# First feed-forward output as seven half-size products, with its input sums made as the input is produced and the modulation sums spread anew

## The chip, the cores and the metric

The kernel runs on one core of one Trainium2 chip. Times are device microseconds (us) of that core, from one launch; lower is better. Clocks inside one profiled execution are counted from the start of its span. Engines are named as in the profile: PE (matrix), PEld (its weight loads), DVE (vector), ACT (scalar), POOL and SP (which here mostly issue DMAs).

## The reference

A two-layer trunk for 256 latent tokens and 256 context tokens of width 1024. Layer 0 mixes tokens with a bidirectional mLSTM, layer 1 with latent attention; each mixer is followed by a gated convolutional feed-forward. In layer 0 both streams are computed, in layer 1 only the latent one is read at the end.

```python
def _conv_ffn(h, w_in, conv_w, conv_b, w_out):
    gate, up = jnp.split(h @ w_in, 2, axis=-1)          # 1024 -> 2 x 2816
    return (jax.nn.silu(_dwconv(gate, conv_w, conv_b)) * up) @ w_out   # 2816 -> 1024
...
for i in range(DEPTH):                                   # DEPTH = 2
    ml = _modulation(c, ada_w[i], ada_b[i])              # six vectors of 1024 per condition
    mc = _modulation(c_ctx[None, :], ada_w[i], ada_b[i])
...
    x = _layer_norm(ALPHA * x + ml[2] * yl, ln_g[i, 0], ln_b[i, 0])
    f = _conv_ffn(_modulate(x, ml[3], ml[4]), ffn_w_in[i], ...)
    x = _layer_norm(ALPHA * x + ml[5] * f, ln_g[i, 1], ln_b[i, 1])
```

The change concerns the last product of layer 0's feed-forward, `(512 tokens x 2816) @ w_out (2816 x 1024)`, for both streams.

## The kernel before

Everything is float32, and each product is made of three matmuls on split operands. `split` turns a tile into a rounded high part (a cast on ACT, `L380`, or `L315` for weights) and a low part (a subtraction on DVE, `L381` or `L318`). `mm3` (`L375` to `L377`) then issues high x high, high x low and low x high into one PSUM tile. The pool of PSUM tiles has eight tiles of 128 x 512, all of one tag.

Weights come through the class `Stream`. `_plan` writes the fixed order of weight tiles (128 x 1024 at most, 512 KB), `_load` issues the DMA of the next one on SP into a ring of raw tiles, `_split` casts and subtracts it into one of three split tiles (`NB = 3`, tag `w`), and `use` hands it to the matmuls. So the split of tile number k waits until the matmuls of tile k-3 have ended. Tiles marked wide are split into tiles of the tag `u` instead, and do not wait for one of the three. From `bufs` on, later stages add further tags to the ring of raw tiles.

The stages, in the order PE runs them: `up` and `og` (projections), `v` (`w_v`, which already is made of seven half-size products in place of eight, with sums of the weights by `_sum` and sums of the input in `x_sums`), `qk` with the heads, `mout` (mixer output), `fin0` (first feed-forward product), `fout0` (its output), then `dkv`, `ukn`, `uv` and the rest of the attention, `aout`, `fin1`, `fout1`.

In `fin0`, `ffn_in` makes 22 pairs of PSUM tiles (gate and up), runs the convolution (`conv`: two ACT steps and two DVE steps), multiplies, and splits the result into the 22 tiles `act`, kept in SBUF. In `fout0`, `outmm` runs over these 22 tiles twice: first for the 256 context tokens (four PSUM tiles: two token blocks by two halves of the width), then for the 256 latent tokens. Each weight tile is thus loaded and split twice and serves 12 matmuls each time. While the latent half runs, the context half goes through residual, LayerNorm and transposes (`after0`, `ln_rows`, `ln_T`) one step per weight tile (`tick`). The last six weight tiles are wide; before them stands `mla_ctx`, which computes the context's `dkv` product from the normalized context (`hc`). After them the latent half goes through the same LayerNorm (`z` tiles, `zT` transposes) while PE runs `ukn` and `uv` of the context; then comes `dkv` of the latent half (`hl`).

The modulation vectors that are not needed at the start are computed on DVE in the background: `ada_all` yields one step at a time, each a multiply with a running sum over a 128 x 1024 tile (`junk<-ar,bc`, `L504`). 128 of these are spread over the stages by the rates `ADA_U` (`up`), `ADA_T` (`og`), `ADA_Q` (`qk`), `ADA_M` (`mout`), `ADA_F` (`fin0`), steps per weight tile.

A scheduler orders the instructions of each engine when the program is built, from the order of issue and its own estimates; at run time each engine works its queue in that order.

Of the kernel before, what the change touches and what calls it, by code (L numbers as in the profile page):

```python
# [7 lines left out]
F32 = mybir.dt.float32  # L8
# [6 lines left out]
D = 1024  # L15
# [23 lines left out]

VE = {1: (3, 0), 2: (3, 0), 3: (3, 0)}  # L40

ADA_U, ADA_T, ADA_Q, ADA_M, ADA_F = 1, 0.8, 1.6, 0.6, 1.3

# [10 lines left out]
TAIL = {"mout": 4, "fout0": 6, "aout": 7, "fout1": 6}  # L54
WIDE = {"mout": 5, "fout0": 6, "aout": 7, "fout1": 10}


def _stat(w, m, kt0, nkt):
# [10 lines left out]
def _plan():  # L69
    ids, order = {}, []  # L70

    def add(key, cols, wide=False):
        if key not in ids:
            ids[key] = (len(ids), cols)
        order.append((key, wide))

    for m in range(16):
        add(("up", m, 0), 1024)
    for s in range(4):
        for c in range(4):  # L80
# [36 lines left out]
    for k in range(8):  # L117
        add(("aout", 0, k), 1024, k >= 8 - WIDE["aout"])
    for p in range(NF):
        add(("fin1", p, 0), 1024, p < 2)  # L120
        add(("fin1", p, 1), 1024, p < 2)
    for k in range(NF):
        add(("fout1", 0, k), 1024, k >= NF - WIDE["fout1"])
    return ids, order


def _pack(i):
# [12 lines left out]
    for key, (n, cols) in ids.items():  # L140
# [4 lines left out]
            b = _mov(i["m_w_og"][0][:, a * 512:(a + 1) * 512], 2 * c, 2)  # L145
        elif kind == "gates":
            b = gz.reshape(16, 128, 16).transpose(1, 0, 2).reshape(128, 256)
        elif kind[0] == "v":

            x, y = {"v11": (0, 0), "vt1": (0, 1), "v21": (1, 0), "vt4": (1, 0)}.get(kind, (1, 1))  # L150
            q = i["m_w_v"][0][:, (2 * a + y) * 512:(2 * a + y + 1) * 512]
            b = np.concatenate([q[k * 128:(k + 1) * 128] for k in (4 * c + x, 4 * c + 2 + x)], axis=1)
        elif kind == "qk":
            b = _stat(i["m_w_qk"][0], a, 8 * c, 8)
        elif kind == "mout":
# [73 lines left out]
class Stream:  # L229


    def __init__(self, k, ids, order, ws):
        self.k, self.ids, self.order, self.ws = k, ids, order, ws
        self.n = len(order)
        self.nl = self.ns = self.nu = 0
        self.live, self.kept = [], []
        self.limit = self.n
        self.raw, self.hl, self.tags = {}, {}, {}
        self.nsum = 0

# [4 lines left out]
        self.bufs.append((keys.index(("fout0", 0, 8)), self.bufs[-1][1] + [("acc", 2)] * 2 + [("ar1", 1), ("junk", 1)]))  # L245
        self.bufs.append((keys.index(("aout", 0, 0)), self.bufs[-1][1] + [("ar", 2)] * 2))

    def ring(self, j):
# [13 lines left out]
    def _load(self):  # L262
        k, j = self.k, self.nl
        key = self.order[j][0]
        n, cols = self.ids[key]
        j0, ring = self.ring(j)
        tag, bufs = ring[(j - j0) % len(ring)]
        t = k.pool.tile([128, CW], F32, tag=tag, name="raw", bufs=bufs)
        if key[0] == "vt4":
            k.nc.sync.dma_start(t, k.t2d[key[1]][key[2]])  # L270
            k.nc.gpsimd.dma_start(t, self.ws[n], accum_op=ALU.add)
        elif key[0] != "vt2":
            k.nc.sync.dma_start(t[:, :cols], self.ws[n, :, :cols])
        self.raw[j] = t
        self.tags[j] = tag
        self.nl += 1

    def _sum(self, j):

        key = self.order[j][0]  # L280
        if key[0] == "vt1":
            nc, pin = self.k.nc, self.k.tc.keep_in_program_order
            t2, b11, b22, b12 = [self.raw[i] for i in range(j - 3, j + 1)]
# [4 lines left out]
    def _split(self):  # L288
# [24 lines left out]
            k.nc.vector.tensor_sub(v[:, :, 1], src, v[:, :, 0])  # L313
        else:
            k.nc.scalar.copy(h[:, :cols], src)  # L315
            if key[0] == "vt2":
                k.nc.scalar.dma_start(k.t2d[key[1]][key[2]], src)
            k.nc.vector.tensor_sub(l[:, :cols], src, h[:, :cols])  # L318
        self.hl[j] = (h, l)
        self.ns += 1  # L320
# [26 lines left out]
class K:  # L347
# [141 lines left out]
    def ada_bg(self, l, c, nconds):  # L489


        nc = self.nc
# [5 lines left out]
        for k in range(8):  # L498
            w = self.art.pop(0)
            self.ar_load()  # L500
            for j in range(nconds):
# [2 lines left out]
                nc.vector.scalar_tensor_tensor(o, w, 1.0, self.bc[j], op0=ALU.mult, op1=ALU.mult,  # L504
                                               accum_out=col[:, k, j:j + 1])
                yield
        b = self.smc("ada_c")[:, 48 * l + 8 * c:48 * l + 8 * c + 8].unsqueeze(2).to_broadcast([128, 8, nconds])
# [21 lines left out]
    def ada_all(self, items):  # L529
# [3 lines left out]
        for j in range(2):  # L533
# [4 lines left out]
        self.arq = [(l, c, k) for l, c in items for k in range(8)]  # L538
        self.art, self.nar = [], 0
        for _ in range(2):  # L540
            self.ar_load()
# [2 lines left out]
        for r in self.bc:  # L544
            nc.scalar.activation(r, r, AF.Silu)  # L545
        yield
        for l, c in items:
            yield from self.ada_bg(l, c, 2 if l == 0 or c < 2 else 1)
        self.bc = None


# [23 lines left out]
    def start_up(self):  # L575
# [5 lines left out]
        self.t2d = [[self.dr.tile([128, 1024], F32, name="t2d%d%d" % (p, j)) for j in range(4)] for p in range(2)]  # L581
# [700 lines left out]
    def ffn_in(self, l, hT, n, nt, pre=()):  # L1282
# [5 lines left out]
        for p in range(NF):  # L1288
# [16 lines left out]
            tmp = self.s2("fg")  # L1305
            self.conv(pss[0], [cw[:, j * NF + p:j * NF + p + 1] for j in range(3)], cb[:, p:p + 1], tmp, n)
            nc.vector.tensor_tensor(tmp[:, :n], tmp[:, :n], pss[1][:, :n], op=ALU.mult)
            a = self.u("act")
# [3 lines left out]
        return acts  # L1312


    def rms(self, ps, n, dst):
# [280 lines left out]
def build(tc, off, a, out):  # L1596
    es = ExitStack()
    with es:
# [4 lines left out]
        k.setup()  # L1603
        st.skip(NUP)
        k.start_up()
        k.bg2.append(k.ada_all(((0, 2),)))
        k.w_up()
        k.bg = [k.x_sums()]
        k.w_og()
# [1 line left out]
            k.step(k.bg2)  # L1611
        k.w_v()
        k.drain()
        k.bg2.append(k.ada_all(((0, 3), (0, 4), (0, 5), (1, 0), (1, 1), (1, 2), (1, 3), (1, 4), (1, 5))))
        gp = k.gates()
        S = None
        tt = None
# [64 lines left out]
        while k.bg2:  # L1682
            k.step(k.bg2)
        h0 = None
        act = lambda i: (acts[i][:, 0], acts[i][:, 1])
        pc = k.acc4()
        xr = k.res_load(x1d, 0)
        gate = k.bcast(k.gd[0, 5][1:2, :], "gate")
        k.outmm("fout0", range(NF), act, pc, 0, NF, 1)
        hcu = [k.u("hc") for _ in range(4)]  # L1690
        hc = lambda i: tuple(hcu[i // 2][:, n, (i % 2) * 256:(i % 2 + 1) * 256] for n in range(2))
        k.bg = [after0(pc, xr, gate, 0, 1, 1, 0, hc, None)]
        pl = k.acc4()
        xr = k.res_load(x1d, 2)
        gate = k.bcast(k.gd[0, 5][0:1, :], "gate")
        k.outmm("fout0", range(NF - TAIL["fout0"]), act, pl, 256, NF, 1)
        k.drain()
        kv0 = [x[0] for x in order].index(("ukn", 0, 0))
        st.limit = kv0 + PA
        k.rope_load()  # L1700
        k.mla_ctx(hc)
        hc = hcu = None
        k.outmm("fout0", range(NF - TAIL["fout0"], NF), act, pl, 256, NF, 1, True)
        acts = None
        hlu = [k.u("hl") for _ in range(4)]
        hl = lambda i: tuple(hlu[i // 2][:, n, (i % 2) * 256:(i % 2 + 1) * 256] for n in range(2))
        x2d = k.dr.tile([2, 128, D], F32, name="x2d")
        k.bg = [after0(pl, xr, gate, 1, 1, 1, 0, hl,
                       [x2d[0], x2d[1]])]
        k.tick(1)  # L1710
        st.pump(kv0 + PB)
        k.tick(1)
# [64 lines left out]
```

## Time and profile before

| | |
|---|---|
| median of 3 runs | 1394.01 us (1393.62 to 1394.03) |
| the profiled execution's own time | 1394.95 us |
| its span | 1393.2 us |
| PE busy | 1368.5 us, 98% |
| DVE busy | 1030.5 us, 74% |
| ACT busy | 694.2 us, 50% |
| mean granted PE clock | 0.997 |

The profiled execution took 0.94 us more than the median, and 1.75 us of it lie outside its span. The ends of matmuls are modelled, so the distance between two starts says more than a duration. In the views by stretch, each engine's busy time in a stretch is followed by its count of instructions, then come the PE clock, the share of the DMA engines and GB/s.

### The profile page before, as it was taken

Reading aid. Unit: us, or ns where it says so; the run is one execution under the profiler, and the core shown is the slowest. Engines: PE = TensorE matmul, PEld = TensorE weight load, DVE = VectorE, ACT = ScalarE, POOL = GpSimd, SP = SyncE. Lnnn points to the kernel's source line nnn. Section 1 sums busy time; section 2 is a strip of 40 time slices with the busy share of each in tenths; the row PEclk is TensorE's granted clock in tenths of the full one; section 3 lists DMA queues with packets and bytes.
Section 4 is the critical chain, followed back from the end, with each engine's and each line's share of the span. In section 5 each row is a group of like instructions: output and inputs, shape, how many; then the busy total and the mean of one; then the engine's idle time right before and its main releaser. Section 6 shows DMA issues by size and latency. Waiting matters only on the chain.

```text
span 1393.2 us, 19087 instructions
## 1 busy us (share of the span) xinstructions
PE 1368.5 (98%) x6969; PEld 1152.3 (83%) x6969; DVE 1030.5 (74%) x1627; ACT 694.2 (50%) x1161; POOL 107.6 (8%) x193
## 2 busy tenths in 40 slices
PE   7999999999999999999999999999999999999997
PEld 3788888888788888878798888888888998999986
DVE  6598657687688697789799777754567889777773
ACT  6585434445544545375654343333464667455560
POOL 0033000011011011110000000000000001000000
PEclk9999999999999999999999999999999999999999
DMA  9688748789655364656737677755565326357650
GB/s 337 225 276 298 263 158 242 243 289 289 228 196 209 110 230 153 222 195 212 252 138 238 225 243 241 251 183 181 187 209 179 137 99 213 108 189 226 210 182 31
DMA packets 91262, 288.97 MB, mean 207 GB/s; under 512 B 11288, under 2 KB 19736, under 8 KB 91168
## 3 DMA queue, kind: packets, MB, share of 16 engines
q1 hardware_dynamic: 69824, 224.29, 48.4%
q0 software_dynamic: 15296, 50.36, 11.5%
q10 hardware_dynamic: 6048, 13.11, 2.5%
q8 instruction: 54, 0.88, 0.3%
q14 instruction: 40, 0.33, 0.1%
HBM read 261.46 MB, written 26.26 MB: 207 GB/s over the span
## 4 chain that ended last, share of the span: by engine, by line
PE 91%; DVE 3%; ACT 2%; DMA 2%; issue 1%; SPq 0%; DVEq 0%; ACTq 0%
PE fin L375 9%; PE fin L376 9%; PE fin L377 9%; PE tok L375 6%; PE tok L377 6%; PE tok L376 6%; PE y L376 5%; PE y L377 5%; PE y L375 5%; PE qk L375 4%; PE qk L377 4%; PE qk L376 4%; PE up L375 2%; PE up L377 2%; PE up L376 2%; DMA raw<-in_ws 2%
## 5 line engine op out<-in xcount | busy, mean ns | idle before, releaser
L318 DVE TENSOR_TENSOR w<-raw,w 128x1024 fp32r<-128x1024 f32 (+2 forms) x289 | 350.7, 1215 | 202.8 <-ACT w L315 202.1
L315 ACT CAST w<-raw 128x1024 fp32r<-128x1024 f32 (+2 forms) x289 | 302.2, 1046 | 345.2 <-PE fin L377 107.0
L376 PE MATMUL fin<-h,w 128*128 128x256 f32 (+1 forms) x696 | 231.7, 333 | 0.0
L377 PE MATMUL fin<-h,w 128*128 128x256 f32 (+1 forms) x696 | 231.4, 333 | 0.0
L375 PE MATMUL fin<-h,w 128*128 128x256 f32 (+1 forms) x696 | 231.3, 333 | 0.1
L504 DVE SCALAR_TENSOR_TENSOR junk<-ar,bc 128x1024 f32<-128x1024 f32 x128 | 155.9, 1218 | 7.5 <-ACT bc L545 5.4
L375 PEld LDWEIGHTS fin<-h,w 128*128 128x128 f32 x696 | 132.1, 190 | 13.2 <-ACT h L1201 0.3
L377 PEld LDWEIGHTS fin<-h,w 128*128 128x128 f32 x696 | 132.2, 190 | 12.9
L376 PEld LDWEIGHTS fin<-h,w 128*128 128x128 f32 x696 | 132.2, 190 | 12.8 <-DVE h L1202 0.2
L375 PE MATMUL qk<-xc,w 128*128 128x512 f32 x256 | 100.7, 393 | 0.0
L377 PE MATMUL qk<-xc,w 128*128 128x512 f32 x256 | 99.9, 390 | 0.0
L376 PE MATMUL qk<-xc,w 128*128 128x512 f32 x256 | 99.8, 390 | 0.0
L375 PE MATMUL y<-w,act 128*128 128x512 f32 (+1 forms) x212 | 80.4, 379 | 0.0
L376 PE MATMUL y<-w,act 128*128 128x512 f32 (+1 forms) x212 | 80.1, 378 | 0.0
L377 PE MATMUL y<-w,act 128*128 128x512 f32 (+1 forms) x212 | 80.0, 378 | 0.0
L375 PEld LDWEIGHTS qk<-xc,w 128*128 128x128 f32 x256 | 48.1, 188 | 10.1 <-issue 0.4
L377 PEld LDWEIGHTS qk<-xc,w 128*128 128x128 f32 x256 | 48.1, 188 | 9.9
L376 PEld LDWEIGHTS qk<-xc,w 128*128 128x128 f32 x256 | 48.1, 188 | 9.7
L318 DVE TENSOR_TENSOR wu<-raw,wu 128x1024 fp32r<-128x1024 f32 x36 | 43.5, 1221 | 13.4 <-ACT wu L315 13.1
L375 PE MATMUL up<-hT,w 128*128 128x512 f32 x128 | 50.4, 394 | 0.5 <-ACT hT L380 0.5
L665 ACT ACTIVATE fg<-fg 128x512 f32<-128x512 f32 (+1 forms) x44 | 23.0, 523 | 55.7 <-DVE fg L663 52.6
L376 PE MATMUL up<-hT,w 128*128 128x512 f32 x128 | 50.1, 392 | 0.5 <-DVE hT L381 0.5
(396 smaller groups left out, 2925.8 us busy)
## 6 DMA issues: line engine op xcount, KB each, us to landing
raw<-in_ws SPq DMA_DIRECT2D x306, 512.0 KB, 4.3
ar<-in_adaT SPq DMA_DIRECT2D x80, 512.0 KB, 4.7
adaw<-in_ada_w SPq DMA_DIRECT2D x32, 256.0 KB, 5.9
xmd<-xr POOLq DMA_DIRECT2D x16, 256.0 KB, 4.5
xcd<-cv POOLq DMA_DIRECT2D x16, 256.0 KB, 4.2
xs<-xmd POOLq DMA_DIRECT2D x16, 256.0 KB, 5.7
od<-o ACTq DMA_DIRECT2D x16, 256.0 KB
t2d<-raw ACTq DMA_DIRECT2D x8, 512.0 KB
```

Source lines behind the costliest of these rows:

```text
L315: k.nc.scalar.copy(h[:, :cols], src)
L318: k.nc.vector.tensor_sub(l[:, :cols], src, h[:, :cols])
L375: mm(out, w[0], x[0], start=start, stop=False)
L376: mm(out, w[0], x[1], start=False, stop=False)
L377: mm(out, w[1], x[0], start=False, stop=stop)
L504: nc.vector.scalar_tensor_tensor(o, w, 1.0, self.bc[j], op0=ALU.mult, op1=ALU.mult, accum_out=col[:, k, j:j + 1])
L665: nc.scalar.activation(tmp[:, :n], tmp[:, :n], AF.Silu)
```

## The change

The 512 x 2816 by 2816 x 1024 product is cut in two along tokens (context, latent), depth (even and odd tiles, 11 each) and width (512 each), and made of seven products of 256 x 1408 by 1408 x 512. In `ffn_in` a new `act_sums` runs once per pair of feed-forward tiles: four sums or differences of 128 x 256, two splits of 128 x 512 (as many as before), and two DMAs on POOL that store three parts unsplit in DRAM (`fd`). A new `w_fout0` runs four products together (`yt2` with S2, `y11` with 1, `yt3` with S3, `yt1` with S1; all eight PSUM tiles), with the sums of weight tiles made by `_sum` on DVE; combines them (`u1` to `u3`, `v`); then `y21`, `y22` and `yt4` one after the other. The parts 2, S4 and 3 of the input come back from DRAM by POOL (`zr`) and are split on ACT and DVE (`fz`). The residual of the finished parts (`residual`) and of each later product (`add`) runs on DVE beside the matmuls. `yt4` takes the sum `t2` that was stored to DRAM, plus a weight tile added by a DMA on POOL. The context half is complete after `y22`; its LayerNorm stands beside the first three tiles of `yt4`, then `mla_ctx`, then the last three (`YTAIL`).

The ring of raw tiles has 11 places from `yt2`, and 7 from `y22`. The modulations: 12 of the 128 steps move from `fin0` to `up`, `og` and `mout`.

```diff
-ADA_U, ADA_T, ADA_Q, ADA_M, ADA_F = 1, 0.8, 1.6, 0.6, 1.3
+ADA_U, ADA_T, ADA_Q, ADA_M, ADA_F = 1.4, 1.3, 1.6, 0.8, 1.05
...
+YTAIL = 3
...
-    for g in range(2):
-        for k in range(NF):
-            if g == 1 and k == NF - TAIL["fout0"]:
-                for c, n in enumerate((3, 3, 2)):
-                    add(("dkv", 0, c), n * 320)
-            add(("fout0", 0, k), 1024, g == 1 and k >= NF - WIDE["fout0"])
+    cols = [1024] * 5 + [512]
+    for j in range(6):
+        for n in ("yt2", "y11", "yt3", "yt1"):
+            add((n, 0, j), cols[j])
+    for n in ("y21", "y22", "yt4"):
+        for j in range(6):
+            if (n, j) == ("yt4", 6 - YTAIL):
+                for c, m in enumerate((3, 3, 2)):
+                    add(("dkv", 0, c), m * 320)
+            add((n, 0, j), cols[j], n == "yt4" and j >= 6 - YTAIL)
...
+        self.bufs.append((keys.index(("yt2", 0, 0)), self.bufs[-1][1] + [("acc", 2)] * 2 + [("ar1", 1), ("junk", 1)] +
+                          [("ar", 2)] * 2 + [("u", NU)] * 2))
+        self.bufs.append((keys.index(("y22", 0, 0)), self.bufs[-1][1][:7]))
...
+    def act_sums(self, j, x1, x2):
...
+        nc.vector.tensor_sub(t[:, a], x1[:, b], x2[:, b])
+        nc.vector.tensor_sub(t[:, b], t[:, a], x1[:, a])
+        nc.gpsimd.dma_start(d[:, 0:512], x2)
+        nc.vector.tensor_sub(x1[:, b], x1[:, a], x1[:, b])
+        u, v = self.u("fa"), self.u("fs")
+        self.split(u[:, 0], u[:, 1], x1)
+        self.split(v[:, 0], v[:, 1], t)
+        nc.vector.tensor_add(x1[:, a], x2[:, a], t[:, b])
+        nc.gpsimd.dma_start(d[:, 512:768], x1[:, a])
...
+    def w_fout0(self, x1d, mid):
...
+        def operand():
...
+                    pin(nc.gpsimd.dma_start(r[:, h * 256:(h + 1) * 256], self.fd[j][:, off[x]:off[x] + 256]))
...
+                pin(nc.scalar.copy(u[:, 0, :n], r[:, :n]))
+                nc.vector.tensor_sub(u[:, 1, :n], r[:, :n], u[:, 0, :n])
...
+        for i in range(6):
+            for name, ps, x in (("yt2", p6, "S2"), ("y11", p1, "1"), ("yt3", p7, "S3"), ("yt1", p5, "S1")):
+                w = st.use((name, 0, i))
+                prod(ps, x, w, i)
...
+                if n >= 10:
+                    operand()
...
+        for b in range(2):
+            u = self.s2("u1")
+            nc.scalar.copy(u, p1[b])
...
+            nc.vector.tensor_tensor(u, p6[b], u1[b], op=ALU.add)
...
+        def residual():
+            for us, g, c in ((u1, 0, lo), (u4, 0, hi), (u3, 1, lo), (vv, 1, hi)):
+                for b in range(2):
+                    zz = z[2 * g + b]
+                    nc.vector.tensor_tensor(us[b], us[b], gate[g][:, c], op=ALU.mult)
+                    nc.vector.scalar_tensor_tensor(zz[:, c], zz[:, c], ALPHA, us[b], op0=ALU.mult, op1=ALU.add)
+                    if us is vv:
+                        nc.vector.bn_stats(stats[2 * g + b][:, 1], zz[:, c])
+                    yield
+        def add(g, c, ps):
+            for b in range(2):
...
+                nc.vector.tensor_tensor(t, ps[b], gate[g][:, c], op=ALU.mult)
+                nc.vector.tensor_tensor(zz, zz, t, op=ALU.add)
+                nc.vector.bn_stats(stats[2 * g + b][:, c.start // 512], zz)
+        self.bg.append(residual())
+        ps = pair()
+        for i in range(6):
+            w = st.use(("y21", 0, i))
+            prod(ps, "2", w, i)
+            self.tick(1)
+            operand()
+        add(0, lo, ps)
+        ps = pair()
+        for i in range(6):
+            w = st.use(("y22", 0, i))
+            prod(ps, "S4", w, i)
+            self.tick(1)
+            operand()
+        self.drain()
+        add(0, hi, ps)
+        self.bg = [mid(0, z[0:2], stats[0:2])]
+        self.step(self.bg)
+        ps = pair()
+        for i in range(6 - YTAIL):
+            w = st.use(("yt4", 0, i))
+            prod(ps, "3", w, i)
+            self.tick(2)
+        self.drain()
+        mid(None, None, None)
+        ws = [(i, st.use(("yt4", 0, i), hold=True)) for i in range(6 - YTAIL, 6)]
+        for b in range(2):
+            for i, w in ws:
+                prod(ps, "3", w, i, (b,))
...
+        self.bg = [mid(1, z[2:4], stats[2:4], lambda: add(1, lo, ps))]
...
-        k.bg2.append(k.ada_all(((0, 2),)))
+        k.bg2.append(k.ada_all(((0, 2, 0, 8), (0, 3, 0, 4))))
```

More of the change, by code (lines that the diff above doesn't have):

```diff
@@ L52 @@
     "S3 20 A3 24 T3 22 23 M3 31 32 33 34 30").split()]
-TAIL = {"mout": 4, "fout0": 6, "aout": 7, "fout1": 6}
-WIDE = {"mout": 5, "fout0": 6, "aout": 7, "fout1": 10}
+TAIL = {"mout": 4, "aout": 7, "fout1": 6}
+WIDE = {"mout": 5, "aout": 7, "fout1": 10}
+YTAIL = 3
 def _stat(w, m, kt0, nkt):
@@ L147, in _pack @@
             b = gz.reshape(16, 128, 16).transpose(1, 0, 2).reshape(128, 256)
[L148 to L152, printed above, removed]
+        elif kind[0] in "vy":
+            x, y = {"11": (0, 0), "t1": (0, 1), "21": (1, 0), "t4": (1, 0)}.get(kind[1:], (1, 1))
+            q = (i["m_w_v"] if kind[0] == "v" else i["ffn_w_out"])[0][:, (2 * a + y) * 512:(2 * a + y + 1) * 512]
+            b = np.concatenate([q[k * 128:(k + 1) * 128] for k in (4 * c + x, 4 * c + 2 + x)[:cols // 512]], axis=1)
         elif kind == "qk":
@@ L268, in _load @@
         t = k.pool.tile([128, CW], F32, tag=tag, name="raw", bufs=bufs)
[L269 to L272, printed above, removed]
+        if key[0] in ("vt4", "yt4"):
+            k.nc.sync.dma_start(t[:, :cols], k.t2d[key[0][0], key[1], key[2]][:, :cols])
+            k.nc.gpsimd.dma_start(t[:, :cols], self.ws[n, :, :cols], accum_op=ALU.add)
+        elif key[0] not in ("vt2", "yt2"):
             k.nc.sync.dma_start(t[:, :cols], self.ws[n, :, :cols])
@@ L280, in _sum @@
         key = self.order[j][0]
-        if key[0] == "vt1":
+        if key[0] in ("vt1", "yt1"):
             nc, pin = self.k.nc, self.k.tc.keep_in_program_order
-            t2, b11, b22, b12 = [self.raw[i] for i in range(j - 3, j + 1)]
+            t2, b11, b22, b12 = [self.raw[i][:, :self.ids[key][1]] for i in range(j - 3, j + 1)]
             pin(nc.vector.tensor_add(b22, b22, b12))
@@ L497, in ada_bg @@
             col = self.modc[l, c][:, :, 0:nconds]
-        for k in range(8):
+        for k in range(k0, k1):
             w = self.art.pop(0)
@@ L537, in ada_all @@
             self.bc.append(r)
-        self.arq = [(l, c, k) for l, c in items for k in range(8)]
+        self.arq = [(l, c, k) for l, c, k0, k1 in items for k in range(k0, k1)]
         self.art, self.nar = [], 0
@@ L546, in ada_all @@
         yield
-        for l, c in items:
-            yield from self.ada_bg(l, c, 2 if l == 0 or c < 2 else 1)
+        for l, c, k0, k1 in items:
+            yield from self.ada_bg(l, c, k0, k1, 2 if l == 0 or c < 2 else 1)
         self.bc = None
@@ L580, in start_up @@
         self.xmd = self.dr.tile([16, 128, 512], F32, name="xmd")
-        self.t2d = [[self.dr.tile([128, 1024], F32, name="t2d%d%d" % (p, j)) for j in range(4)] for p in range(2)]
+        self.t2d = {(n, p, j): self.dr.tile([128, 1024], F32, name="t2d")
+                    for n, a, b in (("v", 2, 4), ("y", 1, 6)) for p in range(a) for j in range(b)}
         self.xA, self.x1, self.xc, self.xcr = {}, {}, [], []
@@ L1307, in ffn_in @@
             nc.vector.tensor_tensor(tmp[:, :n], tmp[:, :n], pss[1][:, :n], op=ALU.mult)
+            if l == 0:
+                if p % 2:
+                    self.act_sums(p // 2, acts.pop(), tmp)
+                else:
+                    acts.append(tmp)
+                continue
             a = self.u("act")
@@ new lines, in z_norm @@
+    def z_norm(self, zs, stats):
+        nc = self.nc
+        for z, st in zip(zs, stats):
+            mv = self.tiny(2, "mv")
+            nc.vector.bn_aggr(mv, st)
+            rs = self.tiny(1, "rs")
+            nc.scalar.activation(rs, mv[:, 1:2], AF.Sqrt, bias=self.keps, scale=1.0)
+            nc.vector.reciprocal(rs, rs)
+            nm = self.tiny(1, "nm")
+            nc.vector.scalar_tensor_tensor(nm, mv[:, 0:1], -1.0, rs, op0=ALU.mult, op1=ALU.mult)
+            nc.vector.tensor_scalar(z[:, 0:512], z[:, 0:512], mv[:, 0:1], rs, op0=ALU.subtract, op1=ALU.mult)
+            nc.scalar.activation(z[:, 512:1024], z[:, 512:1024], AF.Identity, bias=nm, scale=rs)
+            yield
@@ L1613, in build @@
         k.drain()
[L1614 removed]
+        k.bg2.append(k.ada_all([(0, 3, 4, 8)] + [(l, c, 0, 8) for l, c in ((0, 4), (0, 5), (1, 0), (1, 1), (1, 2), (1, 3), (1, 4), (1, 5))]))
         gp = k.gates()
@@ L1684, in build, with half, mid, norm1 @@
         h0 = None
[L1685 to L1689, printed above, removed]
-        hcu = [k.u("hc") for _ in range(4)]
[L1691 to L1701, printed above, removed]
-        hc = hcu = None
[L1703 to L1709, printed above, removed]
+        kv0 = [x[0] for x in order].index(("ukn", 0, 0))
+        hcu = [k.u("hc") for _ in range(4)]
+        hlu = []
+        x2d = k.dr.tile([2, 128, D], F32, name="x2d")
+        def half(us):
+            return lambda i: tuple(us[i // 2][:, n, (i % 2) * 256:(i % 2 + 1) * 256] for n in range(2))
+        hc, hl = half(hcu), half(hlu)
+        def mid(g, zs, stats, first=None):
+            if g is None:
+                st.limit = kv0 + PA
+                k.rope_load()
+                k.mla_ctx(hc)
+                return
+            return norm1(g, zs, stats, first)
+        def norm1(g, zs, stats, first):
+            A, B = k.ln_mod_cols(1, 1, 0, 1 - g)
+            if first is not None:
+                first()
+                hlu.extend([k.u("hl") for _ in range(4)])
+            yield from k.z_norm(zs, stats)
+            yield from k.ln_T(zs, A, B, hl if g else hc, g == 1)
+            if g:
+                k.late.append(k.ln_x(1, zs, [x2d[0], x2d[1]]))
+        k.w_fout0(x1d, mid)
+        hc = hcu = None
         k.tick(1)
```

85 lines of the change are left out of this document (80 added, 5 removed).

## The prediction

> **What bounds the kernel now.** I read the page's busy times and its chain that ended last, then busy time by stage, then PE's waits.
>
> ```profile
> PE 1368.5 (98%) x6969; PEld 1152.3 (83%) x6969; DVE 1030.5 (74%) x1627; ACT 694.2 (50%) x1161; POOL 107.6 (8%) x193
> PE 91%; DVE 3%; ACT 2%; DMA 2%; issue 1%; SPq 0%; DVEq 0%; ACTq 0%
> ```
>
> PE is the bound and the chain is PE: a matmul less is worth its time only if nothing else becomes late instead.
>
> ```profile
> 60.00:121.00 61.00, 61.00 (x271) 50.52 (x270) 49.67 (x72) 44.58 (x81) 15.86 (x29) 1.00 0.82 278
> 121.00:208.00 87.00, 87.00 (x385) 72.03 (x385) 57.34 (x98) 39.29 (x67) 10.34 (x19) 1.00 0.66 234
> 208.00:361.00 153.00, 153.00 (x676) 126.20 (x675) 115.45 (x124) 70.51 (x82) 14.78 (x22) 1.00 0.82 261
> 593.00:685.00 92.00, 90.47 (x424) 73.45 (x423) 77.69 (x139) 57.03 (x106) 8.73 (x16) 1.00 0.68 219
> 685.00:943.00 258.00, 257.10 (x1207) 215.16 (x1206) 197.82 (x299) 104.41 (x184) 13.13 (x24) 1.00 0.66 218
> 943.00:1071.00 128.00, 127.18 (x588) 105.92 (x587) 79.27 (x105) 63.22 (x82) 2.19 (x4) 1.00 0.61 195
> ```
>
> The rows are most of `up`, then `og`, `v`, `mout`, `fin0`, `fout0`; after the length come PE, PEld, DVE, ACT, POOL. In `fout0` PE is full and DVE has 48.7 of 128 us free. `v`, made of seven products already, keeps PE full with DVE at 115.45 of 153. PE's waits in these stages are small:
>
> ```profile
> PE y L376 <- DVE w L318: 1.5, 3, 1.1
> PE ckT L1369 <- DVE ckr L1321: 0.8, 1, 0.8
> ```
>
> **What is removed.** Eight products of 11 depth tiles x 2 token blocks x 3 matmuls are 528 matmuls; seven are 462. The build's order of PE's queue shows 462. Their pace:
>
> ```profile
> 950.27 0.39 PE L375 MATMUL y<-w,act 128*128 128x512 f32 x1
> 952.99 0.39 PE L375 MATMUL y<-w,act 128*128 128x512 f32 x1
> ```
>
> Twelve matmuls (one weight tile) lie between these starts: 2.72 us, 0.2267 each. Removed: 66 x 0.2267 = 15.0 us, all of it on the path.
>
> **What DVE gets.** Its pace when it works without a gap, at start-to-start:
>
> ```profile
> 1001.40 1.22 DVE L318 TENSOR_TENSOR w<-raw,w 128x1024 fp32r<-128x1024 f32 x1
> 1002.53 0.69 DVE L1132 SCALAR_TENSOR_TENSOR z<-xres,z 128x512 f32<-128x512 f32 x1
> 1003.13 0.68 DVE L1131 TENSOR_TENSOR z<-y,gate 128x512 f32<-128x512 f32 x1
> 1003.73 0.68 DVE L1134 BATCH_NORM_STATS2 st<-z 128x6 f32<-128x512 f32 x1
> 1004.34 1.21 DVE L318 TENSOR_TENSOR w<-raw,w 128x1024 fp32r<-128x1024 f32 x1
> 1021.09 0.76 DVE L1202 TENSOR_TENSOR hc<-zm,hc 128x256 fp32r<-128x256 f32 x2 [0.76 <-ACT hc L1201]
> 1065.50 0.68 DVE L1131 TENSOR_TENSOR z<-y,gate 128x512 f32<-128x512 f32 x1
> 1066.22 0.69 DVE L1132 SCALAR_TENSOR_TENSOR z<-xres,z 128x512 f32<-128x512 f32 x1
> ```
>
> So 1.13 us for 1024 columns, 0.60 for 512 (multiply, multiply-add and statistics alike), 0.38 for 256; a step that reads the one just before it starts after 0.72.
>
> `fin0`: 11 x 4 sums of 256 columns add 16.7 us. The number of splits stays. Twelve modulation steps leave, at
>
> ```profile
> L504 DVE SCALAR_TENSOR_TENSOR junk<-ar,bc 128x1024 f32<-128x1024 f32 x128 | 155.9, 1218 | 7.5 <-ACT bc L545 5.4
> ```
>
> 1.22 each, so 14.6 us go. DVE comes to 200 of 258 us: cost 0, hidden behind PE's 257. POOL's 22 new DMAs wait for DVE's steps; behind them in POOL's queue stand only loads for the next stage. Four steps each go to `up`, `og`, `mout`. In `up` and `og` DVE has 11.3 and 29.7 us free for 4.9: cost 0. In `mout` DVE is at 77.69 of 92 and PE already waits 1.5 us for splits; one more step stands ahead of a split there. A split may be some 2.7 us late before PE waits, so I take 0.2, between 0 and 1.2.
>
> Four products together: per group of four weight tiles PE takes 4 x 2.72 = 10.9 us. DVE has 4 splits (4.5), 3 sums (3.4) and, from the third group's end, up to 4 operand splits (2.4): 10.3. It fits, since splits run up to two tiles ahead: cost 0, up to 2 if not.
>
> `y21` and `y22`: here it does not fit. I count from the first matmul of the stage. The four products end at 264 x 0.2267 = 59.8; `y21` and `y22` would end at 89.8. In the build's DVE queue, between the last split of `yt1` and the last of `y22`, stand ten full weight splits and two halves (12.5 us), nine operand splits (7 x 0.60 + 2 x 0.38 = 5.0), eight combinations (4.8), sixteen residual steps with two statistics (10.8) and six steps of `add` (3.6): 36.7 us. What comes first on ACT takes
>
> ```profile
> L315 ACT CAST w<-raw 128x1024 fp32r<-128x1024 f32 (+2 forms) x289 | 302.2, 1046 | 345.2 <-PE fin L377 107.0
> L807 ACT COPY u<-tok 128x512 f32<-128x512 f32 x4 | 2.3, 581 | 1.0 <-PE tok L377 1.0
> ```
>
> 1.05 for a full cast and 0.58 for half of one (the copy's row). `yt1`'s last split cannot end before 57.0: the half-tile three before it ends its matmuls at 246 x 0.2267 = 55.8, then come a half cast and a half split. The first full split finds its buffer free at 57.1 and its cast done some 0.8 after DVE could have begun it. `y22`'s last full split has 1.2 us of those steps after it, so it ends at 57.0 + 0.8 + 36.7 - 1.2 = 93.3; 17 matmuls follow (3.9), and `y22` ends at 97.2 in place of 89.8. Cost 7.4. The largest single wait should be before `y22`'s third tile: ten of those steps (5.7 us) stand between its split and the one before, and a tile lasts 2.72. The handover of PSUM tiles at the start of `y21`, behind the copy of `y11`, is
>
> ```profile
> L810 DVE TENSOR_TENSOR u<-tok,u 128x512 f32<-128x512 f32 x4 | 2.7, 686 | 0.4 <-ACT u L807 0.4
> ```
>
> small in `v` and about 1 us here (it has half-tiles as cover); it lies inside the 7.4, since DVE is the later. Bounds: 4.5 (only demand against supply, any order) to 9 (dependent neighbours, at 0.72).
>
> **The norm of the context** had sixteen weight tiles beside it and has three. After `y22` DVE's queue holds, up to the second normalized tile, seven steps of 512 columns, four weight splits, and short ones: 9.7 us. PE has 3 x 2.72 = 8.2, and waits 1.5 before its transposes. Then ACT must move out eight column blocks, at the pace of
>
> ```profile
> 1078.07 1.02 ACT L1196 ACTIVATE zm<-zT,lnB,lnA 128x256 f32<-128x256 f32 x2 [0.24 <-PE zT L1189]
> 1083.95 2.56 ACT L1201 CAST hl<-zm 128x256 fp32r<-128x256 f32 x8
> 1048.22 0.30 PE L375 MATMUL dkv<-w,hc 128*128 128x320 f32 x1
> 1055.26 0.39 PE L375 MATMUL y<-wu,act 128*128 128x512 f32 x1
> ```
>
> 0.51 + 0.32 = 0.83 per block, against 0.88 for the `dkv` matmuls of one block (7.04 / 8): nearly the same, so only the first block's lag shows. Cost 1.9 in all, between 0 (as now) and 5. Then the first wide split of `yt4` stands behind these casts on ACT: PE waits 1.0 (0 to 2.2). The wait at `ckT`, 0.8 now, finds its data after more matmuls: -0.6.
>
> **The norm of the latents.** Now:
>
> ```profile
> 1073.34 0.28 PE L375 MATMUL kn<-ckT,wu 128*128 128x256 f32 x1
> 1073.66 0.68 DVE L1131 TENSOR_TENSOR z<-y,gate 128x512 f32<-128x512 f32 x1
> 1076.89 0.54 DVE L1162 TENSOR_SCALAR z<-z,mv,rs 128x512 f32<-128x512 f32 x1
> 1076.99 1.48 PE L1189 MATMUL zT<-ident,z 128*128 128x128 f32 x10
> ```
>
> The last product ends at 1073.3, the last tile is normalized 4.1 us later, and 3.65 us of `kn` cover it. In the changed queue three weight splits (of `ukn`, `uv`) stand between those steps, 3.4 us, and DVE starts 0.8 late: some 8 us, of which `kn` in parts covers 4.4. Cost 3.6, between 0 and 5.
>
> **DMA.** `fout0` moves 195 GB/s x 128 us = 25 MB. With the stored sums, parts and residuals I count 35 MB, 290 GB/s over 119 us. The nearest row is `v`: 261 GB/s at share 0.82, PE without a wait. Cost 0, bounded by the fourth rival.
>
> **Sum.** -15.0 + 0.2 + 7.4 + 1.9 + 1.0 - 0.6 + 3.6 = -1.5 us on the span of 1393.2: 1391.7, with the 1.75 us around it 1393.4 against 1394.95 for the profiled run. That run is 0.94 above the median, so the median goes from 1394.0 to 1392.5.
>
> **Rivals.** (1) The two norms stay hidden, as they are now: DVE's queue is not as late there as its order suggests, and only its debt in `y21` and `y22` is paid: -15.0 + 0.2 + 7.4 - 0.6 = -8, 1386.0. For it: no row of `fout0` shows PE waiting for a norm. Against it: the splits between the steps are in the queue.
>
> (2) The new waits lower PE's clock. There is one such place now:
>
> ```profile
> 1190.00:1195.00 5.00, 2.90 (x20) 2.31 (x19) 2.94 (x10) 2.70 (x5) 0.00 (x0) 0.93 0.09 35
> 1195.00:1200.00 5.00, 5.00 (x34) 4.93 (x33) 4.37 (x12) 4.41 (x12) 0.00 (x0) 0.73 0.01 3
> 1073.30:1077.00 3.70, 3.70 (x32) 3.65 (x32) 3.23 (x9) 1.09 (x4) 0.00 (x0) 1.00 0.57 200
> ```
>
> After 2.1 us of idle PE the granted clock is 0.93 and then 0.73 over 5 us each, a loss of 0.07 x 5 + 0.27 x 5 = 1.7 us. In `y22` (one wait of some 3 us), at the context's norm and at the latents' norm waits of this size arise: 3 x 1.7 = 5.1, so 1392.5 + 5.1 = 1397.6, slower than before. It decides from the point where PE idles about 2 us in 5. For it: the row. Against it: in `y22` DVE sets the pace and hides a slower PE, and the 1.1 us waits of `mout` lowered nothing (its row has 1.00).
> The Trainium skill, "TensorE: Matmul & The Clock Gate", Part 1, says the clock falls to half after an idle window of about 3.4 us and returns after a busy one. By that rule waits of 3 us would mostly not lower it, and a fall would cost 3.4 x 0.5 = 1.7 us, an estimate from the page; the trace agrees with the price, but shows a fall after less idle.
>
> (3) The stage does better at both: DVE's debt at its lower bound and the norms at half: -15.0 + 0.2 + 4.5 - 0.6 + 3.2 = -7.7, 1386.3; I count it with (1).
>
> (4) Operands come late: POOL loads parts, gates and residuals in one queue, gates and residuals wait for free tiles, and ACT's cast of a late part holds the weight casts behind it. A load of this size on POOL lands in 5.7 us:
>
> ```profile
> xs<-xmd POOLq DMA_DIRECT2D x16, 256.0 KB, 5.7
> ```
>
> One such hold costs up to 5.7: 1392.5 + 5.7 = 1398.2. In `v` the same kind of load held nothing.
>
> **How the numbers follow.** Forecast 0.45, own range 1389 to 1396; (1) with (3) 0.24; (2) 0.24; (4) 0.07. About 0.2%, 2.8 us, can be told from no change. Of the forecast's 0.45, 0.17 lies below 1391.2, 0.23 within, 0.05 above 1396.8. Faster 0.17 + 0.24 = 0.41, same 0.23, slower 0.05 + 0.31 = 0.36. The range leaves a tenth out at each end: 1385.5 to 1399.
>
> **What would show it.** Right: from `y21` to `y22`'s end DVE without a gap, PE waiting there some 7 us for weight splits, most before the third tile of `y22`; `fin0` with PE full; a wait of 1 to 3 us before each `zT` group. Wrong: DVE gaps in `y22`; clock below 1.00 in this stretch (rival 2); ACT waiting for `zr` DMAs (rival 4); PE waits in `fin0` or in the four products, whose cost I set at nothing.

## The result, and the profile after

The changed kernel takes 1401.66 us (median of 5 runs, 1398.87 to 1403.48) against 1393.62 us before (5 runs, 1393.24 to 1394.03): ratio 1.0054, 95% interval 1.0039 to 1.0070. It is slower by 8 us where 1.5 us less were forecast, and lies above the range. Run again beside the experiments it gave 1401.31 us and 1.0047 (1.0033 to 1.0060; after_again), and 1402.41 us and 1.0058 (1.0046 to 1.0071; after_ctl). The profiled execution, 1403.48 us, is the slowest of its five.

Busy times of the page after, and the chain of work that ended last:

```profile
span 1401.7 us, 19170 instructions
PE 1359.0 (97%) x6903; PEld 1142.3 (81%) x6903; DVE 1074.7 (77%) x1726; ACT 699.5 (50%) x1179; POOL 139.0 (10%) x248
PE 44%; DVE 4%; DMA 3%; ACT 1%; issue 1%; POOL 0%; DVEq 0%; ACTq 0%; POOLq 0%; SPq 0%
```

PE has its 66 matmuls less (6969 to 6903), but its busy time fell by only 9.5 us where 15.0 us of matmuls went: part of the rest ran on a lower clock. PE's share of the chain reads 44% in place of 91%, but the two can't be set side by side: this page follows the chain back only to 647 us, so its shares add up to little more than half of the span. PE's waits from `mout` to the second norm, from its timeline:

```profile
690.79 0.50 PE L384 MATMUL y<-wu,hn 128*128 128x512 f32 x1 [0.57 <-DVE wu L326]
692.20 0.49 PE L383 MATMUL y<-wu,hn 128*128 128x512 f32 x1 [0.68 <-ACT wu L323]
693.45 0.80 PE L384 MATMUL y<-wu,hn 128*128 128x512 f32 x1 [0.76 <-DVE wu L326]
1007.07 0.50 PE L383 MATMUL y<-w,fz 128*128 128x512 f32 x1 [0.68 <-ACT u L1421]
1017.02 0.50 PE L384 MATMUL y<-w,fz 128*128 128x512 f32 x1 [1.02 <-DVE w L326]
1025.31 0.50 PE L384 MATMUL y<-w,fz 128*128 128x512 f32 x1 [0.95 <-DVE w L326]
1041.34 0.80 PE L384 MATMUL y<-w,fz 128*128 128x512 f32 x1 [10.29 <-DVE w L326]
1063.50 0.41 PE L383 MATMUL dkv<-w,hc 128*128 128x320 f32 x1 [0.69 <-ACT hc L1211]
1080.75 0.39 PE L385 MATMUL kn<-ckT,wu 128*128 128x256 f32 x1 [0.48 <-DVE wu L326]
1083.72 0.78 PE L1199 MATMUL zT<-ident,z 128*128 128x128 f32 x4 [1.75 <-issue]
1085.27 0.39 PE L383 MATMUL kn<-ckT,wu 128*128 128x256 f32 x1 [0.77 <-DVE kn L389]
```

In the kernel before, the end of `mout` has one such wait:

```profile
691.33 0.51 PE L376 MATMUL y<-wu,hn 128*128 128x512 f32 x1 [0.76 <-DVE wu L318]
```

Read the waits after by size. One wait of 10.29 us stands out. It is before the third tile of `y22`, exactly where the forecast put the largest one, but it is over three times the 3 us expected there. The row names a weight split on DVE (L326) as the releaser; DVE, ACT and POOL show what held that split, each in its own timeline:

```profile
1028.71 0.68 DVE L1442 SCALAR_TENSOR_TENSOR z<-z,u 128x512 f32<-128x512 f32 x1
1036.73 1.03 DVE L1374 TENSOR_TENSOR fz<-zr,fz 128x512 fp32r<-128x512 f32 x2 [7.34 <-ACT fz L1373]
...
1040.07 1.22 DVE L326 TENSOR_TENSOR w<-raw,w 128x1024 fp32r<-128x1024 f32 x1
1036.08 0.92 ACT L1373 CAST fz<-zr 128x512 fp32r<-128x512 f32 x2 [7.12 <-DMA zr<-fd]
1003.24 1.08 POOL L1367 DMA_DIRECT2D zr<-fd  x2 [1.41 <-DVE fz L1374]
1025.77 0.90 POOL L279 DMA_DIRECT2D raw<-in_ws  x1 [21.45 <-DVE w L326]
1026.35 1.95 POOL L1367 DMA_DIRECT2D zr<-fd  x3
```

From the bottom: POOL stands for 21.45 us at L279, the accumulate DMA of `yt4`'s first tile, which waits for its ring place and for the stored sum to be loaded into it. Behind it in the same queue stand the last three loads of `zr` parts, issued at 1026.35; ACT's cast of them starts at 1036.08, some 8 to 10 us later (the median from issue to landing is 6.0 us for these loads). ACT waits 7.12 us, DVE 7.34 us, and the split that PE needs stands behind DVE's step. The parts are operands of `yt4`'s last tiles, and `yt4` follows `y22`; its first matmul starts at 1052.11 us: nothing needed them yet.

In two more profiles of the same kernel (after_again and after_ctl) the picture is the same but the sizes are smaller: ACT is held for 5.6 and 5.5 us, and PE waits 8.73 and 8.71 us.

The clock, by windows of the kernel after (after the length come PE, PEld, DVE, ACT, POOL, then PEclk, DMA share and GB/s):

```profile
694.00:696.00 2.00, 2.00 (x6) 1.58 (x5) 1.56 (x3) 0.73 (x2) 0.00 (x0) 0.50 0.85 199
1042.00:1044.00 2.00, 2.00 (x6) 1.59 (x5) 2.00 (x3) 0.00 (x0) 0.00 (x0) 0.50 0.77 238
1044.00:1046.00 2.00, 2.00 (x9) 1.60 (x8) 2.00 (x5) 0.45 (x1) 0.00 (x0) 0.81 0.64 165
1046.00:1048.00 2.00, 2.00 (x10) 1.68 (x9) 2.00 (x4) 0.18 (x1) 0.00 (x0) 1.00 0.22 88
1087.00:1089.00 2.00, 2.00 (x12) 2.00 (x11) 1.80 (x4) 1.85 (x4) 0.00 (x0) 0.50 0.38 147
```

Behind three of the places (`mout`'s end, `y22`, the latents' norm) PE works at half clock, then returns to 1.00. Over the 10 us from each fall the means at the first and the last are 0.83, a loss of 1.7 us each. In `y22` the matmuls start 0.43 us apart in place of 0.2267 from 1041.9 to 1044.5, some eight of them: 8 x 0.20 = 1.6 us. The fall at `mout`'s end is not in the two other profiles of this kernel, where the clock is 1.00 there; the one in `y22` is in all three.

### The profile page after: what moved, and what is told of

It reads as the page before. It is cut to its first block, busy times and chain, and to the rows that moved or that the text cites. A ratio compares the mean times of both kernels' runs of the same rounds, so it can differ in the third digit from the quotient of the medians.

```text
span 1401.7 us, 19170 instructions
## 1 busy us (share of the span) xinstructions
PE 1359.0 (97%) x6903; PEld 1142.3 (81%) x6903; DVE 1074.7 (77%) x1726; ACT 699.5 (50%) x1179; POOL 139.0 (10%) x248
## 4 chain that ended last, share of the span: by engine, by line
PE 44%; DVE 4%; DMA 3%; ACT 1%; issue 1%; POOL 0%; DVEq 0%; ACTq 0%; POOLq 0%; SPq 0%
PE fin L383 9%; PE fin L384 9%; PE fin L385 9%; PE y L384 4%; PE y L385 4%; PE y L383 4%; DMA raw<-in_ws 2%; DVE w L326 1%; DVE wu L326 1%; DMA zr<-fd 1%; PE s L1721 0%; DMA raw<-t2d 0%; PE dkv L383 0%; PE dkv L385 0%; PE dkv L384 0%
## 5 line engine op out<-in xcount | busy, mean ns | idle before, releaser
L326 DVE TENSOR_TENSOR w<-raw,w 128x1024 fp32r<-128x1024 f32 (+3 forms) x290 | 348.2, 1203 | 165.7 <-ACT w L323 165.0
L323 ACT CAST w<-raw 128x1024 fp32r<-128x1024 f32 (+3 forms) x290 | 300.4, 1037 | 331.1 <-PE fin L385 89.2
L383 PE MATMUL up<-hT,w 128*128 128x512 f32 x128 | 50.5, 394 | 0.5 <-ACT hT L388 0.5
L384 PE MATMUL up<-hT,w 128*128 128x512 f32 x128 | 50.1, 392 | 0.5 <-DVE hT L389 0.5
L385 PE MATMUL up<-hT,w 128*128 128x512 f32 x128 | 50.1, 391 | 0.3 <-DVE w L389 0.3
L383 PE MATMUL tok<-w,hT 128*128 128x512 f32 x128 | 49.8, 389 | 0.0
L384 PE MATMUL tok<-w,hT 128*128 128x512 f32 x128 | 49.8, 389 | 0.0
L385 PE MATMUL tok<-w,hT 128*128 128x512 f32 x128 | 49.8, 389 | 0.0
```

The costliest lines, as they stand in the source:

```text
L383: mm(out, w[0], x[0], start=start, stop=False)
L384: mm(out, w[0], x[1], start=False, stop=False)
L385: mm(out, w[1], x[0], start=False, stop=stop)
```

## The experiments

Theory Q: the order of POOL's queue holds ACT and DVE. Its rivals: DVE's queue is simply too long (D), or the DMA engines are busy and any load lands late (B).

**acc_late** puts the accumulate DMAs behind the parts.

```
# _load, for yt4: kept in a list while parts are left to load
- k.nc.gpsimd.dma_start(t[:, :cols], self.ws[n, :, :cols], accum_op=ALU.add)
+ self.late.append(lambda: k.nc.gpsimd.dma_start(..., accum_op=ALU.add))
# operand(), behind the last load of a part
+ if not parts: st.flush()
```

> The added loads of `yt4`'s stored sums (the accumulate DMAs on POOL) are issued behind the last three loads of `zr` parts instead of ahead of them; nothing else moves. Theory Q (order of POOL's queue): the parts land long before they are cast, ACT's wait of 7.1 us for them goes, PE's wait of 10.3 us before `y22`'s third tile falls to the 2 to 3 us that DVE's queue alone gives, the granted clock stays near 1.00 there: 1401.7 - 7.5 - 2.5 = 1391.7 (1389 to 1394). Theory D (DVE's debt): ACT's wait goes, but DVE's queue is as long as it was; PE's wait keeps at least 8 us: 1399 to 1402. Theory B (the DMA engines are busy, and any load comes late there): the parts land as late as now, 1400 to 1402.

Measured: 1396.04 us (11 runs), 1.0011 (1.0003 to 1.0020), 5.3 us less than the changed kernel's 1401.31 (from another chip; against the kernel before, each on its own chip, the two stand at 1.0011 and 1.0047). PE's largest wait, the queue on POOL, and a window behind the wait:

```profile
1032.62 0.50 PE L395 MATMUL y<-w,fz 128*128 128x512 f32 x1 [3.23 <-DVE w L337]
1005.03 0.55 POOL L1379 DMA_DIRECT2D zr<-fd  x1 [1.23 <-DVE fz L1388]
1023.27 0.90 POOL L286 DMA_DIRECT2D raw<-in_ws  x1 [17.69 <-DMA raw<-t2d]
```

```profile
1034.00:1036.00 2.00, 2.00 (x6) 1.52 (x5) 2.00 (x4) 0.00 (x0) 0.00 (x0) 0.50 0.86 258
```

The parts are issued by 1005 us, 20 us sooner; ACT no longer waits for one, and PE's wait falls from 10.29 to 3.23 us. Q holds; D, which kept 8 us or more, and B fall. The time is 2 us above the interval that Q gave, since the 3.23 us still halve the clock (last row), which I had counted as gone, and since I had counted 7.5 us for a hold that was 5.5 us in the other two profiles.

**no_resid** and **acc_late_no_resid** take DVE's work away in place of the order, and then both.

```
# residual(): both lines left out
- nc.vector.tensor_tensor(us[b], us[b], gate[g][:, c], op=ALU.mult)
- nc.vector.scalar_tensor_tensor(zz[:, c], zz[:, c], ALPHA, us[b], op0=ALU.mult, op1=ALU.add)
```

> Left out: the sixteen multiply and multiply-add steps of the residual (the four outputs of the four products are not added to the stream); the statistics stay, POOL's order stays. DVE has 9.6 us less to do in `y21` and `y22`. Theory D (DVE's debt): PE's wait in `y22` falls under 1 us and the time to 1401.7 - 10.3 - 2.5 - 2 = 1387. Theory Q (order of POOL's queue): the last parts are still issued behind the accumulate DMA and land at the same time, the third split of `y22` still stands behind them, the wait before it stays 7 us or more: 1397 to 1400.

> Both: the accumulate DMAs behind the last loads of parts, and the sixteen residual steps left out (the output lacks them). Theory Q with the forecast's debt: no wait over 1 us in `y21` and `y22`, clock 1.00, only the waits at the start of `fin0` and at the norms are left: 1401.7 - 10.3 - 2.5 - 2.6 = 1386 (1384 to 1388). If it stays over 1390, something else in this stage takes the time.

Measured: 1396.60 us, 1.0017 (1.0007 to 1.0028), and 1389.54 us, 0.9958 (0.9943 to 0.9972). The first row is of no_resid's PE timeline, the second of its waits (us in total, times, longest):

```profile
1037.65 0.79 PE L384 MATMUL y<-w,fz 128*128 128x512 f32 x1 [7.15 <-DVE w L326]
```

```profile
ACT fz L1373 <- DMA zr<-fd: 7.3, 1, 7.3
```

With 9.6 us of DVE's work gone ACT is still held for 7.3 us, and PE still waits 7.15 us in one place, as Q said; D's 1387 is out of reach. The two waits of 1 us in `y21` and at `y22`'s start are gone, and the time is just under Q's interval. So the wait has two parts, POOL's order and DVE's queue, and each kernel takes away one of the two: 7.1 and 3.2 us of the 10.29 in the first profile, and some 5.5 and 3.2 of the 8.7 in the two others, which fits the 5.3 us that acc_late gains in the median. With both away PE has no wait in `y21` and `y22` but the 0.68 us at the start, and the clock stays at 1.00 from 1010 to 1050 us. The time is 1.5 us above the interval: two short waits come instead, for a split of `yt4` and before the context's transposes (0.60 and 1.06 us).

**rate_m2, before_spread, ar_pool, ar_pool2** are on the modulations.

```
rate_m2:        ADA_M, ADA_F = 0.8, 1.05  ->  0.6, 1.2
before_spread:  the kernel before, with the change's rates, ada_bg(l, c, k0, k1, nconds) and item lists
ar_pool:        ar_load: nc.sync.dma_start -> nc.gpsimd.dma_start, in mout
ar_pool2:       the same, in mout and fin0
```

> The rate of modulation steps in `mout` goes back to 0.6 (as before the change) and that in `fin0` is 1.2 in place of 1.05, so some four steps move from `mout` into `fin0`. Theory M (the steps added in `mout` make the first weight tiles of `fin0` late): PE's three waits at the start of `fin0`, 2.0 us in all, fall to the one of 0.8 that the kernel before has: 1401.7 - 1.2 = 1400.5. Rival: they stay, since they come from the loads of the weights, 1401.7. Either way the rest of `fin0` stays without a wait.

> The kernel before with one part of the change alone: the modulations' new rates and their new order of items; eight products as before. Theory M (a modulation step more in `mout` holds the weight loads behind its own load on SP's queue): PE waits 2.0 us in place of 0.8 for the first `wu` splits at the end of `mout`, the granted clock falls for 10 us behind it, and the time grows by 1.2 + 1.7 = 2.9 us to 1396.6. Theory of the forecast (0.2 us for `mout`, nothing elsewhere): 1393.9.

> The changed kernel with its own rates, but in `mout` the loads of the modulations' weights (`ar`) go through POOL's queue in place of SP's, where the loads of `mout`'s weights stand behind them; the modulation steps stay where they are on DVE. Theory S (the `ar` load waits on SP for its place and holds the weight loads): PE's three waits at the end of `mout`, 1.8 to 2.0 us, fall to 0.8 or less, 1401.3 - 1.2 - 1.7 = 1398.4. Theory V (the step itself makes DVE's splits late, and with them the places of the weight loads): the waits stay at 1.8 to 2.0 us, 1401.3.

> As ar_pool, but every `ar` load from `mout` to the end of `fin0` goes through POOL's queue; in ar_pool the load at 674.6 us, the one between the weight loads that came late, was still on SP's. Theory S (that load on SP holds the weight loads): PE's waits at the end of `mout`, 1.8 to 2.9 us in the runs so far, fall to 0.8 or less, and the time to 1397 to 1399 (1.003 times the kernel before). Theory V (the modulation steps on DVE make the splits late, and these free the places of the loads): the waits stay at 1.8 us or more, 1401 to 1404 (1.0055).

Measured: rate_m2 1397.89 us, 1.0025 (1.0015 to 1.0035); before_spread 1395.64 us, 1.0015 (1.0007 to 1.0024); ar_pool 1403.90 us, 1.0073 (1.0059 to 1.0087), beside the changed kernel's 1402.41 us on that chip (after_ctl); ar_pool2 1403.35 us, 1.0071 (1.0058 to 1.0085). In rate_m2 one wait of 0.27 us is left at `mout`'s end and the clock stays at 1.00 there, a gain of 3.4 to 3.8 us, more than theory M's 1.2. A fall of the clock does not explain the excess: in after_again the clock stays at 1.00 at `mout`'s end too, and yet its first matmul of `fin0` starts 4.5 us later than in rate_m2 (702.77 against 698.24 us), while its listed waits in `mout` are only 2.3 us longer (0.3 us of the difference stood already at 600 us). The rest of that difference stays open. Alone, on the kernel before, the new spread costs 2.0 us in the median and makes three waits at the same place (0.61, 0.75 and 0.77 us); the fall of the clock that I had expected there does not come (1.00). Before `mout` nothing is lost: the two kernels reach 600 us within 0.1 us of each other, and `fin0` starts 1.8 us later with the new spread (701.84 against 700.08). So the steps added to `mout` are the cause, and what they cost is ten times the 0.2 us of the forecast or more.

That the modulations' own loads hold the weight loads on SP, as I had expected, is wrong: with none of them left on SP in this stretch (ar_pool2), PE still waits 2.31 us. What the weight loads do wait for is seen in DVE's and SP's timelines of that run:

```profile
656.54 1.21 DVE L326 TENSOR_TENSOR w<-raw,w 128x1024 fp32r<-128x1024 f32 x1
657.77 0.33 SPq L281 DMA_DIRECT2D raw<-in_ws  x1
659.46 1.21 DVE L326 TENSOR_TENSOR w<-raw,w 128x1024 fp32r<-128x1024 f32 x1
660.70 0.33 SPq L281 DMA_DIRECT2D raw<-in_ws  x1
```

Each load is issued within 0.05 us of the end of a split, which frees its place. A step more ahead of a split on DVE makes the load later, and so a tile several places on: the ACT casts of the `wu` tiles then wait for their DMAs. That this chain makes the 2 us is argued from these rows; it was not tried by itself. Why ar_pool is 1.5 us slower still than the changed kernel beside it stays open.

**combo1 and combo2.** combo1 joins acc_late and rate_m2. combo2 also shortens DVE's queue in `y21` and `y22`:

```
 y21:  self.tick(1)  ->  if i >= 2: self.tick(1);   operand()  ->  operand(load=True, pop=(i == 5))
 y22:  self.tick(1)  ->  if i >= 2: self.tick(1);   operand()  ->  if i >= 1: operand()
 vv's residual: from the queue of y21 and y22 to one beside the dkv matmuls (v gets a buffer of its own)
```

> The changed kernel once more, on the chip of the three runs beside it, so that their times can be set against its own: 1.0054 times the kernel before, as before, and PE's waits of 2.0 us in all at the end of `mout` and of 10.3 us in `y22`.

> The accumulate DMAs behind the last loads of parts (as in acc_late) and the rates 0.6 in `mout` and 1.2 in `fin0` (as in rate_m2), both together. If the two causes are separate, their gains add: the 5.6 us of the one and the 3.8 of the other, from 1401.7 to 1392.3 (1390.5 to 1394); PE keeps one wait of 3.2 us in `y22`, three of about 1 us at the start of `y21`, and 3.0 us at the norm of the latents. If both only removed the same fall of the clock: 1395 to 1396.

> As combo1, and DVE's queue of `y21` and `y22` made shorter: the splits of five of the six last parts, which `yt4` alone needs, are made in `y22` in place of `y21`; the residual begins two tiles later; its last quarter (`vv`, 4 steps and 2 statistics) is made beside the `dkv` matmuls. Theory D for what is left (DVE's debt, 5.9 us of waits and a clock fall of 1.7 us behind the largest): the waits in `y21` and `y22` fall to 2 us or less, the clock stays at 1.00 there: 1392.3 - 3.9 - 1.7 = 1386.7 (1385 to 1389), faster than the kernel before by 0.5%. Rival: the steps come back as a later norm of the context (they stand in DVE's queue beside it), 1389 to 1392.

Measured on one chip: the changed kernel 1401.31 us; combo1 1392.12 us, 0.9986 (0.9977 to 0.9994); combo2 1387.75 us, 0.9954 (0.9939 to 0.9969). The gains of the two causes add, as combo1's interval said: 5.3 and 3.4 us make 8.7, and 9.2 were found. combo2 lies inside its theory's 1385 to 1389 too. PE's largest wait in `y21` and `y22` and the one in `yt4`, in combo2, and windows of this stage:

```profile
1009.28 0.50 PE L395 MATMUL y<-w,fz 128*128 128x512 f32 x1 [0.81 <-DVE w L337]
1041.10 0.50 PE L395 MATMUL y<-w,fz 128*128 128x512 f32 x1 [1.58 <-DVE w L337]
```

```profile
1020.00:1030.00 10.00, 10.00 (x46) 8.29 (x45) 10.00 (x15) 4.70 (x7) 1.75 (x2) 1.00 0.80 215
1030.00:1040.00 10.00, 9.52 (x42) 7.54 (x41) 8.73 (x15) 5.52 (x7) 0.90 (x2) 1.00 0.88 272
1068.00:1072.00 4.00, 3.53 (x17) 3.20 (x16) 2.29 (x8) 2.25 (x5) 0.00 (x0) 0.50 0.58 177
```

`y21` and `y22` run almost full, the largest wait in `y22` is gone, and combo2 is faster than the kernel before by 0.46%. Part of it comes back: a wait of 1.58 us for a split of `yt4`, and at the latents' norm, whose waits are as in the changed kernel, the clock is at half again (last row).

## Why the prediction was wrong, by its own steps

The three signs against it in `y22` all came: a gap of 7.34 us on DVE, the clock at 0.50, and ACT waiting 7.12 us for `zr` loads.

- **What is removed, -15.0.** 6903 matmuls remain, 66 fewer. Once the two causes below are taken out, combo1's median of 1392.12 us stands beside the forecast of 1392.5. That they agree so closely is partly luck: the sum has no term for the 1.7 us of half clock that combo1 keeps in `y22`, and takes 2.2 us too much for the context's norm.
- **DMA, cost 0: the step that failed.** I counted bytes (290 GB/s against `v`'s 261) and took the time from the share of the DMA engines. What counted was one queue's order: a load that waits for a place stood ahead of three loads that could have gone. Rival 4 names the mechanism ("ACT's cast of a late part holds the weight casts behind it"), but I set its price at one landing, 5.7 us, and its chance at 0.07, arguing that in `v` the same kind of load held nothing. It could not have: the loads of parts (`xs`) are all issued by 169.3 us, and `v`'s first accumulate comes at 227.97; only stores stand behind the accumulates there. That an accumulate holds its queue could be read in the kernel before, in `v`:

```profile
305.38 0.90 POOL L271 DMA_DIRECT2D raw<-in_ws  x1 [18.03 <-DMA raw<-t2d]
```

  The hold on ACT is 5.5 to 7.1 us in the three profiles of the changed kernel, and nothing covers it, since DVE was already in debt there. It comes to 5.3 us in the median. So the price of rival 4 was about right; what failed is the zero in the sum, and the chance.
- **`mout`, 0.2 between 0 and 1.2: failed.** 2.0 us on the kernel before, 3.4 to 3.8 on the changed one. I asked how late one split may be, not when it frees the place of a later load.
- **`y21` and `y22`, 7.4: right.** Without POOL's hold (acc_late) the waits are 0.68, 1.03, 0.94 and 3.23 us; the place and size of the largest were as forecast. By starts, `yt4`'s first matmul comes 98.9 us after the stage's first, against 89.8 without any debt: 9.1, of which 1.7 are half clock, and 7.4 are left.
- **The clock, rival 2: right in kind.** Its price of 1.7 us a place is what the rows show (1.6 in `y22`), but it does not exclude the other cases; it comes on top of each. It does not come every time: of its three places, none at the context's norm, `y22` in all three profiles, the latents' norm in two. My argument against it, that DVE hides a slower PE in `y22`, is not borne out: behind the large wait PE has no other in `y22`, so the matmuls at half clock are on the path.
- **Norm of the context, 1.9, and `yt4`'s resume, 1.0: too much.** PE waits 0.69 us before `dkv` and not at `yt4`. The `ckT` wait of 0.8 us is gone (-0.6 was taken).
- **Norm of the latents, 3.6: right.** 0.48 + 1.75 + 0.77 = 3.0 us. The row names no releaser for the 1.75; DVE's queue has the second normalized tile at 1083.09, just before `zT`, behind the splits, as forecast.
- **`fin0` and the four products, cost 0: right.** No wait in either before 1007 us.

On the profiled run the account closes within 1 us: -15.0, waits in `y21` and `y22` +12.9, `mout` +1.25, context +0.7, `ckT` -0.8, latents +3.0, three falls of the clock +5.0, and 0.7 us more at the kernel's start, in all +7.7 against the +8.5 us of the spans.

The Trainium skill, "TensorE: Matmul & The Clock Gate", Part 1, says that the clock is either full or half, that it falls after an idle window of about 3.4 us, returns after a busy one, and that the window runs freely. This case agrees on half clock (0.50 in the rows), on the price and on the free window, but not on how much idle time it takes: in the changed kernel waits of 2.0 us within 3 us at `mout`, and of 1.75 us before `zT` with two short ones beside it, are followed by half clock, while in acc_late waits of 1.76 and 1.75 us at the same places leave it at 1.00. My 0.93 and 0.73 over 5 us each were means over such a fall, not its depth.

## What to carry to other kernels

Walk each DMA queue in order as you walk an engine's: for every issue, ask what it waits for and which issue behind it could go now; a load that waits for a buffer belongs behind the loads that are ready, and the split of an operand belongs behind the splits that are needed sooner (combo2 did this together with two other moves, so its own worth is not shown). A queue's hold and an engine's debt at the same place add up, so test each alone and then both. A new wait on PE can bring half clock behind it, 1.7 us here: the waits of 3.23 us and more in `y22` did in every profile, groups of some 2 us in some and not in others, so give that term a chance and not a fixed price.

## What the runs showed of the hardware

I had not expected waits of one length at one place to have two prices: 1.75 us before the latents' transposes was followed by half clock in the changed kernel and in combo2, and by full clock in acc_late and in combo1. The clock's records in the traces show what differs. In each of the thirteen traces the clock changes only at instants that lie a multiple of 3.41 us apart, and a fall that ends inside the span lasts 3.41, 6.83 or 10.24 us. What goes with a fall is the idle time of PE inside one such stretch, not the length of a wait. The stretches around `mout`'s waits, in the changed kernel (two rows) and in acc_late (two rows); PE's busy time stands behind the length:

```profile
689.78:693.19 3.41, 1.66 (x5) 0.48 (x3) 1.97 (x2) 1.66 (x3) 0.00 (x0) 1.00 0.66 219
693.20:696.61 3.41, 3.16 (x8) 2.51 (x9) 2.70 (x5) 1.91 (x2) 0.00 (x0) 0.50 0.85 252
```

```profile
688.64:692.05 3.41, 2.35 (x9) 1.17 (x8) 2.75 (x3) 2.57 (x5) 0.00 (x0) 1.00 0.57 199
692.05:695.46 3.41, 2.71 (x13) 1.99 (x12) 2.42 (x4) 1.33 (x2) 0.00 (x0) 1.00 0.89 291
```

In the first, 1.75 us of idle time lie in one stretch and the next one runs at half clock; in the second, waits of nearly the same total are split 1.06 and 0.70 between two stretches, and the clock stays. Over all traces, from 25 to 1380 us, a stretch at full clock with 1.99 us of waits or more was always followed by half clock, one with 1.58 or less never; between 1.60 and 1.89 us both occur. Where a group of waits falls against these stretches changes from one execution to the next, so part of such a price is luck.

The wait in `y22`, 3.23 us or longer where it is there at all, had half clock behind it in every profile. The second surprise is the queue: three loads of 128 KB that were ready stood some 20 us behind one that was not, on an engine that was busy for 10% of the span.
